# Constant products on TensorE, a gain loaded earlier, and another order of transposes in a two-block transformer kernel

## The chip, the cores and the metric

The kernel runs on one core of one Trainium2 chip. The time is that of the device for one execution, in microseconds (us); the time before is the median of 3 runs. A profile shows one execution: its span is the time from the first to the last instruction. Engines are named as in the profile: PE (TensorE, products), PEld (its weight loads), DVE (VectorE), ACT (ScalarE), POOL (GpSimd), SP (SyncE, which issues most transfers).

## The reference

256 tokens of width 1024 pass through two blocks of two layers each. The parts that matter here:

```python
def rms_norm(x, gain):
    xf = x.astype(jnp.float32)
    y = xf * lax.rsqrt(jnp.mean(xf * xf, axis=-1, keepdims=True) + NORM_EPS)
    return (y * gain.astype(jnp.float32)).astype(x.dtype)

def swiglu(h, w_gate, w_up, w_down):
    return (jax.nn.silu(h @ w_gate) * (h @ w_up)) @ w_down
...
def second_block(x, ...):
    for l in range(DEPTH):
        ...
        mix = jnp.concatenate([o_gla, o_rwkv, o_nsa], axis=-1) @ w_out[l]
        x = _layer_norm(DEEPNORM_ALPHA * x + mix, ln1_w[l], ln1_b[l])

        ffn = (jax.nn.silu(x @ ffn_w_gate[l]) * (x @ ffn_w_up[l])) @ ffn_w_down[l]
        x = _layer_norm(DEEPNORM_ALPHA * x + ffn, ln2_w[l], ln2_b[l])
    return x
```

The first block begins each layer with half a feed-forward (`x + swiglu(rms_norm(x)) / 2`), then a mixer and attention to a memory, then another half feed-forward. The second block has a mixer and a feed-forward per layer, each followed by a layer norm.

## The kernel before

x stays in SBUF as two tiles of 128 tokens (token half 0 and 1, `self.x[h]`), 1024 wide. Every product is taken in three: each f32 operand is split into a rounded part (`hi`) and the rest (`lo`). For weights, ACT writes `hi` (L159) and DVE `lo` (L160), one 512 KB tile at a time, out of four buffers that SP fills.

`norm_T` (L277) turns x into an operand. It takes x in four pieces, a token half h and a half i of the width; each piece is multiplied by the gain if there is one (L292), transposed by four PE transposes into one PSUM bank (L231), and split by ACT (L234) and DVE (L235). The order is i outside, h inside. Where there is a gain, ACT also sums squares (L300), and POOL takes the power that gives the root mean square (L244); the scaling itself comes after the product. `ffn1` (four calls, L365) and both mixers of block one call it with a gain; `ffn2` (two calls, L1041) and `mixer2` (two calls, L1114) call it without.

The very first thing that the program does with data is `ffn1(0, 0)`: `load_consts` (L380) issues the first part of the constants (identity and the exponent) on ACT's queue, `load_x` (L401) four loads of x on SP's, and `row_gain` (L247) two loads of the gain, spread over 128 partitions, through `load` (L172), which is POOL's queue at that point. Then come the feed-forward's weight tiles on SP's.

In block two, `post` (L1021) makes the layer norm: as the last product of each token half ends, DVE adds it to x (L1033) and takes statistics (L1035), then `ln` (L1007) makes the norm: DVE L1011 and L243, POOL's power L244, DVE L1016 twice, and DVE L1019 twice, of which each finishes one half of the width. Half 0 ends its last product first, so its norm runs under PE's products of half 1; the norm of half 1 has no products beside it. `swiglu` (L322) then takes the operand of both halves at once (256 columns, L480), 24 products to a weight tile; `dense` (L197) takes each token half by itself (512 columns, L217 to L219).

The order of every engine's queue is laid out by a planner that runs the program through a model, takes at each point the instruction that is ready and has the lowest priority number (`cur_priority`, counted up in program order), and gives out buffers. `later(n)` moves the instructions inside it n places back, and with a negative n forward; `norm_T` moves the two pieces with i = 0 forward by `AHEAD` = 150. On the chip each queue is then run in that order.

Of the kernel before, what the change touches and what calls it, by code (L numbers as in the profile page):

```python
# [18 lines left out]
AF = mybir.ActivationFunctionType  # L19
OP = mybir.AluOpType  # L20
# [4 lines left out]
def bcast_rows(ap, n, offset=0, parts=128):  # L25
    return bass.AP(tensor=ap.tensor, offset=ap.offset + offset, ap=[[0, parts], [1, n]])


class Core:
# [191 lines left out]
                    done(h, o)  # L221


    def split_T(self, src, nb, put):

        nc = self.nc
        for b0 in range(0, nb, 4):
            m = min(4, nb - b0)
            pt = self.p("t")
            for i in range(m):  # L230
                nc.tensor.transpose(pt[:, i * 128:(i + 1) * 128], src[:, (b0 + i) * 128:(b0 + i + 1) * 128], self.ident)  # L231
            v = pt[:, :m * 128].rearrange("p (b t) -> p b t", b=m)
            hi, lo = put(b0, m)
            nc.scalar.activation(hi, v, AF.Copy)  # L234
            nc.vector.tensor_tensor(lo, v, hi.bitcast(F32), op=OP.subtract)  # L235


    def rstd(self, ss, n, mean_scale, eps, r=None):
# [8 lines left out]
    def row_gain(self, ap, n):  # L247

        g = (self.kept("g1", 256) if n <= 256 else self.tagged("g4", 1024))[:, :n]
        for n0 in range(0, n, 512):  # L250
            self.load(g[:, n0:min(n, n0 + 512)], bcast_rows(ap, min(512, n - n0), n0))
        return g

    def operand(self, nb, groups=None):
# [19 lines left out]
        t = self.l(512)  # L274
        return [t[:, :256], t[:, 256:]]

    def norm_T(self, xs, gain, gates=True):  # L277


        nc = self.nc  # L280
        ahead = self.AHEAD if gates else 0
        with self.later(-ahead):
            put, get = self.operand(8, [("opX", 4)] * 2 if "opX" in self.caps[0] else None)
            ss = [self.t(2) for _ in range(2)]
        for i in range(2):

            with self.later(0 if i else -ahead):
                for h in range(2):
                    y = x = xs[h][:, 512 * i:512 * i + 512]
                    if gain is not None:  # L290
                        y = self.t(512)
                        nc.vector.tensor_tensor(y, x, gain[:, 512 * i:512 * i + 512], op=OP.mult)  # L292

                    old = self.bank
                    if "pC0" in self.caps[1]:
                        self.bank = f"C{2 * i + h}"
                    self.split_T(y, 4, lambda b, m: put(h, 4 * i + b, m))
                    self.bank = old
                    if gain is not None:
                        nc.scalar.activation(self.t(512), x, AF.Square, accum_out=ss[h][:, i:i + 1])  # L300
        if gain is not None:
            get.r = []
            for h in range(2):
                nc.vector.tensor_tensor(ss[h][:, :1], ss[h][:, :1], ss[h][:, 1:], op=OP.add)
                get.r.append(self.rstd(ss[h][:, :1], 1, 1.0 / 1024, 1e-6, self.l(1)))
            if gates:
                self.gate = self.pow
        return get
# [56 lines left out]
    def ffn1(self, layer, j):  # L365
        nc, I = self.nc, self.I
        gain = self.row_gain(I["ffn_norm"][layer, j], 1024)
        xT = self.norm_T(self.x, gain)
        half = [self.l(1) for _ in range(2)]
        for h in range(2):  # L370
            nc.vector.tensor_scalar(half[h], xT.r[h], 0.5, None, op0=OP.mult)

        def done(h, n0, ps):
            x = self.x[h][:, n0:n0 + 512]
            nc.vector.scalar_tensor_tensor(x, ps, half[h], x, op0=OP.mult, op1=OP.add)  # L375

        self.swiglu(xT, I["ffn_gu"][layer, j], I["ffn_w_down"][layer, j], done)


    def load_consts(self, cp):  # L380

        c = self.consts.tile([128, FIRST], F32, name="cf")
        self.nc.scalar.dma_start(c, cp[:, :FIRST])
        self.c = {k: c[:, a:a + n] for k, (a, n) in CONST_AT.items() if a < FIRST}
        self.ident = self.c["ident"]
        self.mhalf = self.c["mhalf"]

        self.ones = self.consts.tile([128, 160], F32, name="ones")[:, :128]
        self.nc.gpsimd.memset(self.ones, 1.0)

    def load_masks(self, cp, cb):

        c = self.consts.tile([128, CONST.shape[1] - FIRST], F32, name="cp")
        self.load(c, cp[:, FIRST:])
        b = self.consts.tile([128, CONST_B.shape[1]], BF, name="cb")
        self.load(b, cb)
        self.c.update({k: c[:, a - FIRST:a - FIRST + n] for k, (a, n) in CONST_AT.items() if a >= FIRST})
        self.cb = {k: b[:, a:a + n] for k, (a, n) in CONST_B_AT.items()}
        self.ident_b = self.cb["ident"]
# [69 lines left out]
FIRST = CONST_AT["ntri"][0]  # L469
# [535 lines left out]
class Mix2(Mix1):  # L1005
# [34 lines left out]

    def ffn2(self, layer):  # L1041
        I = self.I
        xT = self.norm_T(self.x, None)
        self.post("ln2", layer, "g2", lambda done: self.swiglu(
            xT, I["ffn_gu_2"][layer], I["ffn_w_down_2"][layer], done))

# [850 lines left out]
```

## Time and profile before

| | |
|---|---|
| median of 3 runs | 1983.48 us (1981.07 to 1987.65) |
| profiled execution | 1982.18 us, span 1980.5 us |
| mean granted TensorE clock | 0.985 of full speed |

How to read what follows: times are us from the start of the span. A row of the order of time gives the start, the duration (of all, where several are merged), the engine, the line, the operation, output and inputs, and in brackets how long the engine stood before it and who ended that. The granted clock is a share of 2.4 GHz; 0.50 is 1.2 GHz.

### The profile page before, as it was taken

The numbers are of one execution on the slowest core, as the hardware profiler recorded it, in microseconds if no ns is written. First come the engines' busy times: TensorE is split into PE (matmuls) and PEld (weight loads), VectorE is DVE, ScalarE is ACT, GpSimd is POOL, SyncE is SP. The second block draws the span as 40 slices with busy tenths as digits, with TensorE's granted clock in tenths as the row PEclk, the third lists the DMA queues.
The fourth block names the chain that finished last, engine by engine and source line by source line (L and its number), as shares of the span: only waits on it lengthen the run. The fifth ranks groups of instructions, "written<-read, shape, count | busy, mean of one in ns | idle before, by whom it ended". The sixth has DMA issues, their size and how long they took to land.

```text
span 1980.5 us, 35270 instructions
## 1 busy us (share of the span) xinstructions
PE 1896.3 (96%) x14108; PEld 1683.8 (85%) x14108; DVE 1249.6 (63%) x1999; ACT 995.6 (50%) x1611; POOL 189.9 (10%) x270
## 2 busy tenths in 40 slices
PE   7999999899999999898999999998999997998998
PEld 7998778799989987677999898777998885778996
DVE  5665865766566657766666557666555666665555
ACT  5544655555454545655554455543544464434542
POOL 0000401000000001320000013220000213210000
PEclk9999999999999999999999999999999998989999
DMA  6666443466556656224566654214666654015664
GB/s 231 193 215 223 141 145 106 128 197 194 193 198 192 193 191 201 95 100 139 164 196 194 205 152 140 96 44 144 197 193 193 173 158 132 23 64 180 193 192 138
DMA packets 158645, 319.17 MB, mean 161 GB/s; under 512 B 28944, under 2 KB 49680, under 8 KB 158480
## 3 DMA queue, kind: packets, MB, share of 16 engines
q1 hardware_dynamic: 157888, 315.79, 50.8%
q8 instruction: 111, 1.82, 0.4%
q0 software_dynamic: 160, 0.52, 0.1%
q10 hardware_dynamic: 432, 0.60, 0.1%
q14 instruction: 54, 0.44, 0.1%
HBM read 315.82 MB, written 1.05 MB: 160 GB/s over the span
## 4 chain that ended last, share of the span: by engine, by line
PE 48%; issue 4%; DVE 4%; ACT 1%; DMA 1%; POOL 0%; SPq 0%; DVEq 0%; POOLq 0%; ACTq 0%
PE pd L480 21%; PE pd L218 5%; PE pd L217 5%; PE pd L219 5%; PE po L480 2%; PE pr L480 1%; DVE wl L160 1%; PE ppC L480 1%; PE pr L1477 1%; PE pg L1247 1%; DMA wr<-in_ffn_w_down_dram 1%; PE pq L1477 1%; PE pg L480 1%; PE pt L516 1%; PE pn L480 1%
## 5 line engine op out<-in xcount | busy, mean ns | idle before, releaser
L160 DVE TENSOR_TENSOR wl<-wr,wh 128x1024 fp32r<-128x1024 f32 (+2 forms) x557 | 675.9, 1216 | 394.3 <-PE pd L218 127.4
L159 ACT ACTIVATE wh<-wr 128x1024 fp32r<-128x1024 f32 (+2 forms) x557 | 584.4, 1051 | 553.6 <-PE pd L480 200.8
L480 PE MATMUL pd<-opX,wl 128*128 128x256 f32 x2112 | 585.2, 278 | 2.4 <-DVE s L243 1.0
L480 PE MATMUL pd<-olX,wh 128*128 128x256 f32 x2112 | 585.3, 277 | 0.3 <-DVE olX L235 0.2
L480 PE MATMUL pd<-opX,wh 128*128 128x256 f32 x2112 | 584.5, 277 | 0.0
L480 PEld LDWEIGHTS pd<-opX,wl 128*128 128x128 f32 x2112 | 398.2, 189 | 3.3 <-ACT opX L234 2.2
L480 PEld LDWEIGHTS pd<-olX,wh 128*128 128x128 f32 x2112 | 398.5, 189 | 0.7 <-DVE olX L235 0.7
L480 PEld LDWEIGHTS pd<-opX,wh 128*128 128x128 f32 x2112 | 398.5, 189 | 0.0
L218 PE MATMUL pd<-wl,op 128*128 128x512 f32 (+4 forms) x952 | 366.2, 385 | 3.7 <-DVE wl L160 3.4
L219 PE MATMUL pd<-wh,op 128*128 128x512 f32 (+4 forms) x952 | 362.8, 381 | 0.0
L217 PE MATMUL pd<-wh,ol 128*128 128x512 f32 (+4 forms) x952 | 342.9, 385 | 3.9 <-DVE ol L235 2.9
L218 PEld LDWEIGHTS pd<-wl,op 128*128 128x128 f32 x952 | 179.7, 189 | 39.4 <-DVE wl L160 6.8
L217 PEld LDWEIGHTS pd<-wh,ol 128*128 128x128 f32 x952 | 178.6, 189 | 39.0 <-DVE ol L235 3.6
L219 PEld LDWEIGHTS pd<-wh,op 128*128 128x128 f32 x952 | 179.8, 189 | 32.2
L244 POOL TENSOR_TENSOR ls<-s,cf 128x1 f32<-128x1 f32 (+2 forms) x30 | 26.3, 879 | 719.9 <-DVE s L243 719.9
L357 DVE TENSOR_TENSOR b<-pd,b 128x256 f32<-128x256 f32 x132 | 55.9, 424 | 62.2 <-ACT b L356 44.2
L244 POOL TENSOR_TENSOR s<-s,cf 128x1 f32<-128x1 f32 (+2 forms) x22 | 22.4, 1018 | 441.1 <-DVE s L243 439.7
L356 ACT ACTIVATE b<-b 128x256 f32<-128x256 f32 x88 | 36.7, 418 | 46.6 <-DVE b L355 46.5
L361 DVE TENSOR_TENSOR ol<-b,op 128x512 fp32r<-128x512 f32 x66 | 45.4, 687 | 18.0 <-ACT op L360 18.0
L360 ACT ACTIVATE op<-b 128x512 fp32r<-128x512 f32 x66 | 41.7, 632 | 21.8 <-DVE b L357 21.1
L355 DVE TENSOR_TENSOR b<-pd,lb 128x256 f32<-128x256 f32 x88 | 37.1, 422 | 13.3 <-PE pd L480 13.3
L300 ACT ACTIVATE b<-x 128x512 f32<-128x512 f32 x32 | 20.2, 631 | 39.0 <-DVE x L375 20.9
(551 smaller groups left out, 2347.0 us busy)
## 6 DMA issues: line engine op xcount, KB each, us to landing
wr<-in_ffn_gu_dram SPq DMA_DIRECT2D x264, 512.0 KB, 4.2
wr<-in_ffn_w_down_dram SPq DMA_DIRECT2D x132, 512.0 KB, 3.7
wr<-in_w_in_dram SPq DMA_DIRECT2D x45, 512.0 KB, 4.1
wr<-in_ab_w_in_dram SPq DMA_DIRECT2D x24, 512.0 KB, 4.0
wr<-in_xm_w_kv_dram SPq DMA_DIRECT2D x16, 512.0 KB, 3.7
wr<-in_w_out_dram SPq DMA_DIRECT2D x16, 512.0 KB, 4.2
wr<-in_ab_w_out_dram SPq DMA_DIRECT2D x8, 512.0 KB, 3.6
wr<-in_xm_w_q_dram SPq DMA_DIRECT2D x8, 512.0 KB, 4.0
```

The costliest lines, as they stand in the source:

```text
L159: nc.scalar.activation(hi, raw, AF.Copy)
L160: nc.vector.tensor_tensor(lo, raw, hi.bitcast(F32), op=OP.subtract)
L217: nc.tensor.matmul(o, xl, wh[:, k], start=first, stop=False)
L218: nc.tensor.matmul(o, xh, wl[:, k], start=False, stop=False)
L219: nc.tensor.matmul(o, xh, wh[:, k], start=False, stop=last)
L244: self.pow = nc.gpsimd.tensor_tensor(r, a, self.mhalf[:, :n], op=OP.pow)
L355: nc.vector.tensor_tensor(s, ps[:, :256], R, op=OP.mult)
L357: nc.vector.tensor_tensor(y[:, b * 256:b * 256 + 256], ps[:, 256:], s, op=OP.mult)
L360: nc.scalar.activation(hi, yv, AF.Copy)
L361: nc.vector.tensor_tensor(lo, yv, hi.bitcast(F32), op=OP.subtract)
L480: i = self.k.nc.tensor.matmul(out, lhsT, rhs, start=start, stop=stop, skip_group_check=skip)
L1477: last = nc.tensor.matmul(out[rows(c), i], lhs[rows(c), i], rhs[rows(c), i], start=True, stop=True)
```

## The change

Three things change. First, the first call of `row_gain` issues its loads on ACT's queue, and the constants' first part is issued there between the gain's two loads, not ahead of them. Second, `norm_T` can be told to put products on PE whose results nobody reads: `busy` multiplies constants into a bank that is kept for it. The first norm gets 14 of them (`ones` times `ones`, 128 columns) at its start and 3 behind each of its four groups of transposes; `ffn2` gets 20 (identity times masks in bf16, 512 columns) behind its second group. They are put 20 places back in the plan, except for the 14, and each is laid behind the one before it on PE, the first of a group behind the last transpose. Third, where `norm_T` has no gain, in `ffn2` and `mixer2`, the pieces are taken with h outside and i inside, so that both of token half 0 come first, and it is these two that are moved forward by 150.

```diff
+    def busy(self, n, after=None):
+
+        nc = self.nc
+        for _ in range(n):
+            if self.idle_b:
+                i = nc.tensor.matmul(self.idle, self.ident_b, self.masks[:, :512], start=True, stop=True)
+            else:
+                i = nc.tensor.matmul(self.idle[:, :128], self.ones, self.ones, start=True, stop=True)
+            if after is not None:
+                self.tc.add_manual_dep(i.ins, after.ins.name,
...
+            after = i
...
     def row_gain(self, ap, n):
...
         for n0 in range(0, n, 512):
-            self.load(g[:, n0:min(n, n0 + 512)], bcast_rows(ap, min(512, n - n0), n0))
+            part, src = g[:, n0:min(n, n0 + 512)], bcast_rows(ap, min(512, n - n0), n0)
+            if self.first is None:
+                self.load(part, src)
+            else:
+
+                self.nc.scalar.dma_start(part, src)
+                if n0 == 0:
+                    self.first()
+        self.first = None
...
-    def norm_T(self, xs, gain, gates=True):
+    def norm_T(self, xs, gain, gates=True, fill=()):
...
-        for i in range(2):
-
-            with self.later(0 if i else -ahead):
-                for h in range(2):
...
+        fill = list(fill)
+        if fill:
+            self.idle = self.psum("d")
+            self.idle_b = gain is None
+            if gain is not None:
+                self.busy(fill.pop(0))
+
+        order = [(i, h) for i in range(2) for h in range(2)] if gain is not None else [(i, h) for h in range(2) for i in range(2)]
+        for n, (i, h) in enumerate(order):
+
+            with self.later(0 if n > 1 else -ahead):
...
+                last = self.split_T(y, 4, lambda b, m: put(h, 4 * i + b, m))
+                self.bank = old
+                if n < len(fill):
+                    with self.later(20):
+                        self.busy(fill[n], last)
...
-        xT = self.norm_T(self.x, gain)
+        xT = self.norm_T(self.x, gain, fill=(14, 3, 3, 3, 3) if layer + j == 0 else ())
...
-        self.nc.scalar.dma_start(c, cp[:, :FIRST])
+        self.first = lambda: self.nc.scalar.dma_start(c, cp[:, :FIRST])
...
+        self.masks = b
...
-        xT = self.norm_T(self.x, None)
+        xT = self.norm_T(self.x, None, fill=(0, 20))
```

## Rows read from the trace of the kernel before

**Rows 1.** The page, part 1: busy time, share of the span, instructions.
```profile
PE 1896.3 (96%) x14108; PEld 1683.8 (85%) x14108; DVE 1249.6 (63%) x1999; ACT 995.6 (50%) x1611; POOL 189.9 (10%) x270
```
**Rows 2.** The chain that ended last: start, duration, what; products of layer 1.
```profile
1791.13 121.06 PE pd L480 x1056
```
**Rows 3.** In order of time: the start, all engines, cut.
```profile
0.81 0.41 ACTq L383 DMA_DIRECT2D cf<-in_constants_dram  x1
...
0.82 1.81 SPq L405 DMA_DIRECT2D x<-in_x_dram  x4
...
1.36 1.30 POOL L173 DMA_DIRECT2D g<-in_ffn_norm_dram  x2 [0.34 <-issue]
2.67 3.20 SPq L141 DMA_DIRECT2D wr<-in_ffn_gu_dram  x4
3.77 0.63 ACT L300 ACTIVATE b<-x 128x512 f32<-128x512 f32 x1 [1.24 <-DMA x<-in_x_dram]
...
7.91 1.29 DVE L292 TENSOR_TENSOR b<-x,g 128x512 f32<-128x512 f32 x2 [6.73 <-DMA g<-in_ffn_norm_dram]
...
12.00 1.05 ACT L159 ACTIVATE wh<-wr 128x1024 fp32r<-128x1024 f32 x1
...
14.37 0.58 PE L480 MATMUL pd<-opX,wl 128*128 128x256 f32 x1 [0.64 <-DVE wl L160]
...
19.00 0.28 PE L480 MATMUL pd<-opX,wl 128*128 128x256 f32 x1
```
**Rows 4.** In order of time: block two's feed-forward, layer 0, cut.
```profile
1357.07 0.60 PE L231 MATMUL pt<-cf,x 128*128 128x128 f32 x4
...
1362.74 2.82 PE L231 MATMUL pt<-cf,x 128*128 128x128 f32 x12 [5.08 <-DVE x L1019]
1363.90 0.60 ACT L234 ACTIVATE opX<-pt 128x512 fp32r<-128x512 f32 x1 [5.09 <-PE pt L231]
1364.53 0.69 DVE L235 TENSOR_TENSOR olX<-pt,opX 128x512 fp32r<-128x512 f32 x1 [1.18 <-ACT opX L234]
...
1365.79 0.41 PE L480 MATMUL pd<-olX,wh 128*128 128x256 f32 x1
...
1367.27 0.28 PE L480 MATMUL pd<-opX,wh 128*128 128x256 f32 x1
```
**Rows 5.** Windows: stretch, length, busy per engine, clock, DMA share, GB/s.
```profile
1360.40:1360.60 0.20, 0.00 (x0) 0.00 (x0) 0.17 (x2) 0.00 (x0) 0.00 (x0) 0.55 0.83 307
```
**Rows 6.** In order of time: layer 1's third and fifteenth product, PE.
```profile
1791.36 0.41 PE L480 MATMUL pd<-olX,wh 128*128 128x256 f32 x1
...
1793.92 0.28 PE L480 MATMUL pd<-opX,wh 128*128 128x256 f32 x1
```
**Rows 7.** Landing after issue: first gain load, then first two weight tiles.
```profile
DMA to landing us min/median/max: 6.5/6.5/6.5
...
DMA to landing us min/median/max: 8.3/8.6/9.0
```
**Rows 8.** Windows of the start; the last two columns are DMA share, GB/s.
```profile
3.00:4.00 1.00, 0.00 (x0) 0.00 (x0) 0.00 (x0) 0.23 (x1) 0.00 (x0) 1.00 1.07 396
4.00:5.00 1.00, 0.00 (x0) 0.00 (x0) 0.00 (x0) 1.00 (x4) 0.00 (x0) 1.00 1.14 213
5.00:6.00 1.00, 0.00 (x0) 0.00 (x0) 0.00 (x0) 0.12 (x2) 0.00 (x0) 1.00 0.69 141
```
**Rows 9.** The chain that ended last, inside layer 1's norm of half 1.
```profile
1784.63 0.60 DVE olX L235
```
**Rows 10.** In order of time: mixer of block two, layer 1, cut.
```profile
1553.79 1.28 DVE L235 TENSOR_TENSOR ol<-pr,op 128x512 fp32r<-128x512 f32 x2
...
1554.94 0.48 PE L217 MATMUL pd<-wh,ol 128*128 128x512 f32 x1
```
**Rows 11.** Windows of block two's mixers: stretch, length, PE busy, and so on.
```profile
1136.00:1357.50 221.50, 212.47 (x2055) 175.16 (x2053) 145.88 (x325) 109.40 (x247) 50.50 (x76) 0.98 0.38 107
1547.00:1782.00 235.00, 217.08 (x2052) 178.07 (x2051) 152.43 (x334) 109.50 (x248) 53.47 (x80) 0.95 0.36 103
```

More of the change, by code (lines that the diff above doesn't have):

```diff
@@ L221, in dense @@
                     done(h, o)
+    idle = None
+    def busy(self, n, after=None):
[7 more added lines that the diff above has]
+                self.tc.add_manual_dep(i.ins, after.ins.name,
+                                       mybir.DependencyInfo(mybir.DependencyClass.NoSync, mybir.DependencyReason.DATA),
+                                       reason="while it would wait")
+            after = i
     def split_T(self, src, nb, put):
@@ L230, in split_T @@
             for i in range(m):
-                nc.tensor.transpose(pt[:, i * 128:(i + 1) * 128], src[:, (b0 + i) * 128:(b0 + i + 1) * 128], self.ident)
+                last = nc.tensor.transpose(pt[:, i * 128:(i + 1) * 128], src[:, (b0 + i) * 128:(b0 + i + 1) * 128], self.ident)
             v = pt[:, :m * 128].rearrange("p (b t) -> p b t", b=m)
@@ L235, in split_T @@
             nc.vector.tensor_tensor(lo, v, hi.bitcast(F32), op=OP.subtract)
+        return last
     def rstd(self, ss, n, mean_scale, eps, r=None):
@@ L284, in norm_T @@
             ss = [self.t(2) for _ in range(2)]
-        for i in range(2):
-            with self.later(0 if i else -ahead):
-                for h in range(2):
[L289 to L300, printed above, removed]
+        fill = list(fill)
[7 more added lines that the diff above has]
+            with self.later(0 if n > 1 else -ahead):
+                y = x = xs[h][:, 512 * i:512 * i + 512]
+                if gain is not None:
+                    y = self.t(512)
+                    nc.vector.tensor_tensor(y, x, gain[:, 512 * i:512 * i + 512], op=OP.mult)
+                old = self.bank
+                if "pC0" in self.caps[1]:
+                    self.bank = f"C{2 * i + h}"
+                last = self.split_T(y, 4, lambda b, m: put(h, 4 * i + b, m))
[3 more added lines that the diff above has]
+                        self.busy(fill[n], last)
+                if gain is not None:
+                    nc.scalar.activation(self.t(512), x, AF.Square, accum_out=ss[h][:, i:i + 1])
         if gain is not None:
```

## The prediction

> **What bounds the kernel now.** I read the page first: TensorE (PE) is busy for 96% of the span [rows 1], so only stretches in which it stands still, or runs slower than it can, are worth anything. Next came the list of who waited for whom, for PE alone: its longest waits are that for the first norm's product with the gain, and twice 5.1 us for the layer norm ahead of the second block's feed-forward. These three places are the ones that the change touches, and I read each in the order of time.
>
> *The start* [rows 3]. The first half of x is there at 3.77 us, when ScalarE (ACT) squares it. The gain's first half, issued by POOL at 1.36, is used by VectorE (DVE) at 7.91 only. The first real product starts at 14.37, behind the split of the first weight tile, which ACT begins at 12.00. Then 22 products start over the 4.63 us up to 19.00, 0.21 us apart; after that they come 0.115 us apart, as in the rest of the kernel, where 1056 take 121.06 us [rows 2]. So up to 19.00 PE runs at 1.2 GHz by its pitch and afterwards at 2.4, although the clock column shows 1.00 from the first slice on; here I go by the pitch.
>
> *The feed-forward of block two, layer 0* [rows 4]. PE transposes the first part of token half 0 at 1357.07 and then waits until 1362.74, because the next transposes in its queue belong to token half 1, whose norm ends last. In the pause the granted clock falls to half (0.55 over the slice at 1360.4 [rows 5]). Twelve transposes then take 2.82 us, and the products run 0.21 us apart until the tenth, at 1367.27. *Layer 1* is the same; its clock returns at the fifteenth product [rows 6].
>
> **The change, part by part.**
>
> *First norm's weight loaded first.* It moves two 256 KB loads from POOL's queue to ACT's, ahead of and behind the constants' first part. ACT then issues three transfers instead of one, 0.41 us each by the one row there is [rows 3], from 0.81 to about 2.05. Behind them it has a table load and then waits for x until 3.77 (1.24 us of waiting in that row), which covers the 0.8 us added; without that cover ACT would be 0.8 late. What the gain takes on ACT's queue no row shows. Bounds: x's first half, issued at 0.82 by SP, is used 2.95 us later; the gain on POOL's queue landed 6.5 us after its issue [rows 7]. I take 3.3, near x, which starts at the same time on the same kind of queue: the gain is there at 4.1 rather than 7.9.
>
> That doesn't yet start the products: the first weight tile landed 8.3 us after its issue at 2.67, at 11.0 [rows 7]. The DMA moved 396 GB/s in the fourth microsecond but 213 and 141 in the next two [rows 8], while POOL's two loads were under way. Were these two at 396, 0.44 MB or 1.1 us would be won: the tile lands at 9.9. If the loads are also served in the order of their need, 2.2 MB (x, gain, constants, tile) lie ahead; by an estimate 0.2 MB of it are moved by 3.0 us, and the rest at 396 GB/s is there at 8.0. I take the middle, 8.9. From the start of its split to the first product it is 2.37 us (12.00 to 14.37), so the first product is at 11.3: **-3.1 us**. Bounds: -1.0 if the tile lands at 11.0 as before (13.4), -3.5 if ACT's own work, four squares and two evictions at some 0.6 to 0.8 us behind a second half of x near 6 us, holds the split until 8.5.
>
> The Trainium skill (DMA: Bandwidth & Descriptors, section "Issuing engines are not separate DMA queues") speaks against a gain here: loads from all issuing engines share the same 16 DMA engines and interleave, so another queue saves issue time only. By it the tile would land at 11.0 and this part give the 1.0 us of the bound; the thin slices of rows 8 are why I don't take it whole.
>
> *Products of constants at the start.* 14 products of `ones` run as soon as POOL's memset is done, before POOL's next instruction at 1.36. The nearest row at the low clock is twelve 128-column f32 transposes in 2.82 us [rows 4], 0.23 each: 3.2 us, to 4.6. The first transposes can't start before 4.8 (gain 4.1, DVE's product 0.7), so the 14 lie in a wait. Four times 3 more follow the transposes, 2.8 us at the low clock, while PE waits for DVE and ACT; without that cover they would cost 0.7 a group. PE then works through most of 1.4 to 11 us. In rows 4 the clock came back 4.5 us after the first work behind the pause; so I expect 2.4 GHz before 11.3. The 22 products then take 22 x 0.115 = 2.5 us, not 4.63: **-2.1 us**; bounds 0 and -2.1.
>
> The Trainium skill (TensorE: Matmul & The Clock Gate, section "Part 4: PE-mode transpose") says that transposes don't count as work for the clock in the way products do. By it only the products of constants would work for the clock here, and the -2.1 us would be lost. In rows 4 the full clock came 1.5 us after the third product, in rows 6 2.6, both behind twelve transposes in a row; at the start, with transposes only thinly before, it came 4.6 us after the first. I read that as transposes that counted.
>
> *Token half 0 first, and 20 products behind it.* In the feed-forward PE now transposes both parts of half 0 (8 in about 1.1 us at full clock, to 1358.2), then runs 20 products of 512 columns. Such bf16 products have no row; by the 256-column pitch doubled each takes 0.23, together 4.6 us, to 1362.8. If each took half that, they end at 1360.5 and PE stands for 2.8 us, where the clock may fall and half of the gain below is lost. If each took twice that (half clock throughout) they overrun to 1367.4. I take 0.23, the nearest.
>
> What it costs: evicting the second part adds one DVE subtraction (L235) inside the layer norm of half 1. The chain of waits shows that norm as unbroken DVE work, with the first part's L235 in it at 0.60 us [rows 9]; one more puts 0.60 us on it, unless the planner places it behind. So the first x of half 1 is ready at 1363.3, after the products of constants. Four transposes at full clock end near 1363.9, ACT's eviction (0.60) at 1364.6, DVE's L235 (0.69) at 1365.3. The third product, the first that needs L235's output, starts at 1365.35 (1365.79 before), the tenth 7 x 0.115 later, at 1366.15 instead of 1367.27: -1.1. Layer 1, shifted alike: third at 1790.92 (1791.36), fifteenth 12 x 0.115 later at 1792.30 instead of 1793.92: -1.6. **Together -2.7 us**; bounds -3.9 (L235 behind the norm) and, should only the order work, about 0.
>
> *The mixers of block two* take the order without products of constants. In layer 1 two evictions came in one batch behind the layer norm: DVE's pair began at 1553.79, its first was done at about 1554.45, but PE had four more transposes queued and began at 1554.94 [rows 10]. With half 0 done early only half 1 is left there: **-0.4 us**, bounds -0.9 and +0.6 (L235 again). Layer 0 has no layer norm ahead: 0, bounds -0.6 and +0.6.
>
> One PSUM bank of the feed-forwards is held while the products of constants run; four or five others rotate two at a time, so this costs nothing, and one wait for a bank (up to a 0.4 us product) a group if they didn't.
>
> Sum: -3.1 - 2.1 - 2.7 - 0.4 = **-8.3 us**. Against the profiled execution (1982.18, of which the span is 1980.5) that is 1973.9; that execution lies 1.3 below the median of the runs, so I forecast 1983.5 - 8.3 = 1975.2, **1975** for the median.
>
> **Rivals.**
> - *The weights set the start* (the bound of rows 7): -1.0 there, so -6.2, 1977.3. For it: the weight tiles are three quarters of what the queues hold. Against: the two thin slices.
> - *The clock doesn't come earlier at the start*: -6.2, 1977.3 too. For it: between the groups PE still waits for DVE and ACT; against: rows 4 and 6, as read above.
> - *Products of constants don't hold the clock.* Identity times mask is mostly zeros, and no row shows whether such work counts. Then the clock falls at 1360.4 as before, ten of the 20 are left at 0.46 us, and PE is free at 1365.0 instead of 1362.74: +2.3. Eight transposes instead of twelve follow at 0.23, -0.9: +1.4 in each layer, and nothing from the clock at the start: -3.1 + 2.8 - 0.4 = -0.7, 1982.8, no change that shows.
> - *The planner's order turns worse: slower.* All queues are laid out by one plan over the whole program, and the mixers of block two now give other transposes the priority of 150 places. The two run nearly the same code, yet PE idles 9.0 us in layer 0's stretch and 17.9 in layer 1's [rows 11], so an order can cost up to 8.9 us. If both lost that once, +17.8 - 8.3 = +9.5, 1993.0. It decides from 8.3 us of new PE idle on. For it: this idle is all waits between short steps. Against: the edit inside these stretches is small.
>
> **How the numbers follow.** Chances: forecast 0.47, weights 0.17, clock at the start 0.14, clock not held 0.10, planner 0.12 (either way; slower in 0.07). The likeliest gives 1975. A measurement of this kernel tells about 0.3% (6 us) from no change. Faster: 0.41 of the forecast and half of the two rivals near -6 (0.16): 0.57. Slower: the planner's 0.07. Same: 0.36. The range goes from 1969 (all bounds at their best, -3.5 - 2.1 - 3.9 - 1.5 = -11.0, and 3 us for the scatter of a median) to 1982, which takes in both rivals near -6 and leaves out most of the last two.
>
> **What would show it.** Right: the gain's first use at 4 to 5 us; the first product of L480 near 11.3 and a pitch of 0.115 from there; the clock at 1.00 through both waits; one more L235 in the norm's chain; third products 0.4 us earlier. Wrong: a first weight tile at 11 us; a clock of 0.5 behind the 20 products; transposes of half 1 that stand behind products of constants; more PE idle in a mixer than in rows 11.

## The result, and the profile after

The forecast was 1975 us, range 1969 to 1982. Measured: a median of **1995.45 us** over 20 executions (1983.62 to 2006.28), beside 1984.8 us over 20 for the kernel before on the same chip (1979.21 to 1988.71): a ratio of 1.0053, 95% interval 1.0041 to 1.0065. The change makes the kernel slower by half a per cent, outside my range. Two later measurements of the same kernel gave 1.0031 (1.0012 to 1.0050) and 1.0024 (1.0007 to 1.0041): slower each time, by 4 to 11 us. The changed kernel's executions scatter over 23 us here, those of before over 10; in the two later measurements it is 14 and 13 us beside 20 and 13.

The profiled execution took 1999.06 us, span 1997.3, which is 16.8 us more than before's span. PE's part of the page, beside [rows 1]:

```profile
PE 1923.8 (96%) x14200; PEld 1705.4 (85%) x14200; DVE 1252.9 (63%) x1999; ACT 997.3 (50%) x1611; POOL 183.7 (9%) x268
```

PE is busy 27.5 us longer. The products of constants are some 18 us of that (6.3 for the first 14, some 3 for the next 12, and 2 x 4.5), so other work has become longer too.

*The start*, all engines in order of time, beside [rows 3]:

```profile
0.80 0.41 ACTq L274 DMA_DIRECT2D g<-in_ffn_norm_dram  x1
...
1.06 6.27 PE L233 MATMUL pd<-ones 128*128 128x128 f32 x28 [1.06 <-POOL ones L425]
...
5.29 1.42 DVE L325 TENSOR_TENSOR b<-x,g 128x512 f32<-128x512 f32 x2 [4.12 <-DMA g<-in_ffn_norm_dram]
...
7.17 0.60 PE L248 MATMUL pt<-cf,b 128*128 128x128 f32 x4
...
10.59 1.06 ACT L159 ACTIVATE wh<-wr 128x1024 fp32r<-128x1024 f32 x1
...
13.32 0.39 PE L517 MATMUL pd<-opX,wl 128*128 128x256 f32 x1
```

The gain is used at 5.29 instead of 7.91. The 14 products of constants show as 28 rows and last until 7.33, so that the first transposes wait for them. The first real product starts at 13.32 (14.37 before), and its 0.39 us instead of 0.58 (the row of the low clock in [rows 3]) says that the clock is already full.

*The feed-forward of block two, layer 0*: PE in order of time, beside [rows 4], and a window of it, beside [rows 5]:

```profile
1372.69 1.03 PE L248 MATMUL pt<-cf,x 128*128 128x128 f32 x8
1373.57 4.48 PE L231 MATMUL pd<-cb 128*128 128x512 bf16 x20
1378.96 1.38 PE L248 MATMUL pt<-cf,x 128*128 128x128 f32 x8 [0.92 <-DVE x L1056]
...
1381.03 0.39 PE L517 MATMUL pd<-olX,wh 128*128 128x256 f32 x1 [0.22 <-DVE olX L252]
...
1381.96 0.28 PE L517 MATMUL pd<-opX,wh 128*128 128x256 f32 x1
```
```profile
1377.00:1379.00 2.00, 1.08 (x6) 0.33 (x4) 2.00 (x4) 0.00 (x0) 1.00 (x1) 1.00 1.00 298
```

This place works as forecast: the wait of 5.08 us is 0.92, since 4.48 us of products of constants stand in it, the clock column stays at 1.00, and from the first transposes to the third and the tenth product it is 8.34 and 9.27 us, against 8.72 and 10.20 in [rows 4].

*Inside the feed-forwards* PE is never idle, and yet two of them have become longer. Windows of 80 us in the first one and the two of block two; the bracket behind PE's busy time counts the products:

```profile
40.00:120.00 80.00, 80.00 (x682) 80.00 (x681) 49.99 (x65) 40.00 (x50) 0.00 (x0) 1.00 0.60 187
1390.00:1470.00 80.00, 80.00 (x682) 80.00 (x681) 44.39 (x50) 40.72 (x51) 0.00 (x0) 1.00 0.60 188
1820.00:1900.00 80.00, 80.00 (x708) 80.00 (x707) 46.66 (x54) 41.83 (x55) 0.00 (x0) 1.00 0.61 193
```

682 products in 80 us are one in 117.3 ns, 708 one in 113.0. The same windows of before hold 709, 709 and 708. The clock column is 1.00 in all of them: there are two paces at one clock, which the prediction did not know of.

*The chain that ended last* gives the stretches between. Three pieces of before, then the same three of after; a piece is start, duration, what:

```profile
962.35 107.75 PE pd L480 x951
1365.57 120.56 PE pd L480 x1056
```
```profile
971.83 107.74 PE pd L517 x951
1381.03 124.41 PE pd L517 x1054
1809.91 119.74 PE pd L517 x1054
```

(The third of before is in [rows 2].) From the end of the first piece to the start of the second, the mixer of block two in layer 0 with its norm, it is 295.5 us before and 301.5 after, though the part from the norm's first transposes to the third product is 0.4 us shorter. So the loss has two parts: slow feed-forwards and longer mixers.

### The profile page after: what moved, and what is told of

The parts are those of the page before. It is cut to its first block, busy times and chain, and to the rows that moved or that the text cites. A ratio compares the mean times of both kernels' runs of the same rounds, so it can differ in the third digit from the quotient of the medians.

```text
span 1997.3 us, 35457 instructions
## 1 busy us (share of the span) xinstructions
PE 1923.8 (96%) x14200; PEld 1705.4 (85%) x14200; DVE 1252.9 (63%) x1999; ACT 997.3 (50%) x1611; POOL 183.7 (9%) x268
## 4 chain that ended last, share of the span: by engine, by line
PE 48%; issue 4%; DVE 4%; POOL 1%; ACT 1%; DMA 1%; SPq 0%; DVEq 0%; POOLq 0%; ACTq 0%
PE pd L517 21%; PE pd L217 5%; PE pd L218 5%; PE pd L219 5%; PE po L517 2%; PE pr L517 1%; PE ppC L517 1%; PE pr L1514 1%; DVE wl L160 1%; PE pg L1284 1%; PE pq L1514 1%; PE pg L517 1%; PE pn L517 1%; PE pt L553 0%; PE pq L794 0%
```

## The experiments

Theory A: the products of constants at the start change the planner's order in mixers far behind them, and that costs what is lost. Theory B: the two paces are settled anew in each execution, whatever the kernel. Their rivals stand with each run. The instruction lists of the builds can be compared without the chip: against before, the loads alone change no engine's order behind the first norm. The loads with the 26 products of constants move instructions in the mixers near 250, 860 and 1240 to 1340 us, although no line of code there was touched. The order in which the instructions start in the traces says the same. By that order (it does not tell the pieces of x apart) block two's part alone moves one product near 1145 us and nothing else ahead of layer 0's norm at 1357 us; behind that it moves many, above all from 1665 to 1760 us. e5, e7 and e12 have one list from the first norm on.

The table has the stretches of each trace in us, worked out from the order of time: from the first to the last product of a feed-forward that reads `opX`, and the time between one and the next. "Start" ends with the first product; ff1 is the first feed-forward, ff5 and ff6 those of block two; m0, m1 are the mixers of block one, m2 and m3 those of block two, norms included. The other three feed-forwards are within 0.3 us in all and left out.

| kernel | start | ff1 | m0 | m1 | m2 | ff5 | m3 | ff6 | ratio to before |
|---|---|---|---|---|---|---|---|---|---|
| before | 14.4 | 122.3 | 258.8 | 256.6 | 288.9 | 120.6 | 304.9 | 121.1 | |
| after | 13.3 | 124.8 | 263.4 | 259.6 | 294.5 | 124.9 | 304.0 | 120.2 | 1.0053 |
| e1_again | 12.6 | 120.2 | 260.7 | 258.2 | 296.3 | 120.2 | 305.3 | 120.2 | 1.0031 |
| e2_loads | 12.2 | 122.0 | 261.2 | 254.4 | 289.1 | 120.3 | 304.5 | 121.2 | 0.9984 |
| e3_start | 12.6 | 120.2 | 260.0 | 258.8 | 296.9 | 120.6 | 302.7 | 120.6 | 1.0019 |
| e4_ffn | 13.6 | 121.1 | 260.3 | 257.2 | 288.6 | 120.2 | 302.1 | 120.2 | 0.9976 |
| e5_both | 12.7 | 122.0 | 262.4 | 255.6 | 292.3 | 120.2 | 305.8 | 124.8 | 0.9982 |
| e6_busy_old_loads | 14.6 | 120.2 | 259.7 | 255.8 | 289.1 | 120.4 | 305.7 | 125.3 | 1.0007 |
| e7_four | 12.0 | 126.2 | 261.0 | 253.1 | 288.5 | 120.2 | 301.5 | 124.8 | 0.9975 |
| e8_order_alone | 15.0 | 127.4 | 262.4 | 256.2 | 289.1 | 120.6 | 311.6 | 121.2 | 1.0056 |
| e11_after_again | 12.3 | 120.2 | 260.8 | 257.1 | 297.3 | 120.2 | 303.0 | 120.2 | 1.0024 |
| e12_four_again | 12.2 | 121.9 | 262.4 | 253.1 | 288.5 | 120.2 | 301.7 | 120.2 | 0.9968 |

**e1_again: the changed kernel, unaltered.** No edit.

> The changed kernel unaltered, a second time. Theory A: the two parts of the loss (products 118 instead of 113 ns apart in the first feed-forward and in block two's feed-forward of layer 0; longer mixers, whose instructions stand in another order) belong to the program, so the trace shows the same places again: both streams at 117 to 118 ns, the stretches of mixers within 1 us of the first trace, median 1995. Rival B: the pitch is settled anew in each execution; then another set of the six feed-forwards is slow in this trace (a slow one costs 4.7 us), with the same order of instructions.

Median 1989.94 us, ratio 1.0031 (1.0012 to 1.0050), profiled execution 1988.47. The mixers are long again (m2 296.3), if not within the 1 us that A gave; the feed-forwards are not. The first two of the windows above:

```profile
40.00:120.00 80.00, 80.00 (x709) 80.00 (x708) 51.03 (x65) 40.79 (x51) 0.00 (x0) 1.00 0.62 195
1390.00:1470.00 80.00, 80.00 (x709) 80.00 (x708) 45.61 (x51) 40.69 (x52) 0.00 (x0) 1.00 0.63 196
```

So A holds for the mixers and B for the pace: one program ran the first feed-forward at 682 products in one execution and at 709 in another. Each slow feed-forward costs some 4.7 us (124.9 against 120.2), so such changes may make a part of the scatter; no run shows how large a part.

**e2_loads: only the loads.**

```
-        xT = self.norm_T(self.x, gain, fill=(14, 3, 3, 3, 3) if layer + j == 0 else ())
+        xT = self.norm_T(self.x, gain, fill=())
...
-        order = [(i, h) for i in range(2) for h in range(2)] if gain is not None else [(i, h) for h in range(2) for i in range(2)]
+        order = [(i, h) for i in range(2) for h in range(2)]
...
-        xT = self.norm_T(self.x, None, fill=(0, 20))
+        xT = self.norm_T(self.x, None)
```

> Only the loads in the new order; no products of constants, transposes in the old order. Every engine's order of instructions behind the first norm is then that of before. Theory A: the first weight tile sets the start, -1.0 us there, nothing elsewhere: 1984 beside 1985 for before. Rival (my forecast's step): the tile lands 2.1 us earlier, -3.1 us. Rival B: the stretch lengths of the mixers are as before, but feed-forwards may be slow at random, up to +4.7 each.

Median 1981.22 us, ratio 0.9984 (0.9966 to 1.0002). The start, in order of time, and the landing time of the first weight tile alone (issued at 2.66), beside [rows 7], where it is the 8.3:

```profile
4.87 0.63 ACT L336 ACTIVATE b<-x 128x512 f32<-128x512 f32 x1 [1.37 <-DMA x<-in_x_dram]
...
9.80 1.06 ACT L159 ACTIVATE wh<-wr 128x1024 fp32r<-128x1024 f32 x1
...
12.22 0.58 PE L517 MATMUL pd<-opX,wl 128*128 128x256 f32 x1 [0.29 <-DVE wl L160]
```
```profile
DMA to landing us min/median/max: 7.1/7.1/7.1
```

The first tile now lands at 9.8 instead of 10.9, and ACT begins its split at once, at 9.80; before, the tile had lain there for 1.1 us when ACT came to it, at 12.00. Together that is the 2.15 us by which the first product starts earlier: between the 1.0 that theory A gave and the 3.1 of the forecast. x itself comes 1.1 us later (3.77 before). One start is one draw: in the eight traces with the gain on ACT's queue the tile lands at 9.2 to 10.3 and the first product starts at 12.0 to 13.3, in the four with the old loads at 10.9 to 11.5 and 13.6 to 15.0. The whole time doesn't clear the noise.

**e3_start: loads and products of constants at the start.** The second and third edit of e2 alone.

> The loads and the products of constants at the start, nothing in block two. By the build, the products of constants alone change the order of instructions in the mixers near 250, 860 and 1260 to 1340 us. Theory A: the start -1.0, the first feed-forward slow +2.5, the mixers near 250 and 860 us longer as in the changed kernel (+4.6 and +3.0), a part of the +5.6 near 1300 us: 1992 to 1996. Rival (the order is harmless, block two loses all): 1983.

Median 1988.19 us, ratio 1.0019 (1.0002 to 1.0036): less than theory A gave, which had counted a slow first feed-forward (+2.5) and a longer m0 (+4.6), and neither is in this trace. With ff1 at 120.2, m1 and m2 are 2 and 8 us longer than before, with block two's code untouched. The rival is out: the median is 7 us above that of e2, on the same chip.

**e4_ffn: block two's part alone.** `row_gain` and `load_consts` as before, and the first edit of e2.

> Only block two's part: token half 0 first and the 20 products of constants; loads and start as before. The order of instructions is that of before until 1240 us. Theory A: until then all as before; the mixer of block two in layer 0 up to 3 us longer, its feed-forward slow (+4.2), layer 1 faster (-1.8): 1987 to 1990. Rival (block two's part works as forecast, the loss is all from the start): -2.7, 1982.

Median 1981.31 us, ratio 0.9976 (0.9959 to 0.9994): the rival, my forecast's step, was right. m2 + ff5 + m3 + ff6 come to 831.1 us instead of 835.5. Some 2.4 us of these 4.4 arise at the two norms, as forecast (0.9 and 1.5, below); the rest is in m3, whose order the planner changed.

**e5_both: loads and block two's part, no products at the start.** Only the first edit of e2.

> The changed kernel without its products of constants at the start: the loads and block two's part alone, each 3 to 5 us faster than before by itself. Theory A (the products at the start cost what they cost through the order of the mixer of block two, layer 0): that stretch back to 288 to 290 us instead of 294 to 297, no half clock of 10 us near 1255 and 1340; the two gains add up: 7 us faster than before, ratio 0.9965. Rival (the two parts hinder one another): no faster than either alone, 0.998.

Median 1980.03 us, ratio 0.9982 (0.9964 to 1.0000). The traced execution has one slow feed-forward (124.8) and an m2 of 292.3, longer than A gave but under the 294.5 to 297.3 of the four traces with the changed order. The traced execution is the slowest of the twelve (1991.00 us), and the lists are those of e7 below, whose m2 is 288.5; the same stretch of m2, e5 and then e7, shows why the two differ:

```profile
1143.00:1146.00 3.00, 3.00 (x8) 2.32 (x7) 0.68 (x2) 0.00 (x0) 0.00 (x0) 0.50 0.76 5
```
```profile
1143.00:1146.00 3.00, 3.00 (x17) 2.54 (x16) 1.72 (x2) 1.39 (x2) 0.00 (x0) 1.00 0.26 2
```

In e5 the granted clock falls to 0.50 here and once more near 1273 us, in e7 it doesn't. So at one order a mixer can differ by some 4 us from execution to execution. The median gains 5 us, not 7: by this run alone it is not settled whether the two parts add up.

**e6_busy_old_loads: the 26 products at the start, the gain on POOL's queue.** `row_gain` and `load_consts` as before, and the last two edits of e2.

> The same 14 and 12 products of constants at the start, but the two loads of the gain stay on POOL's queue; block two as before. By the build this changes the order of instructions in the mixer near 250 us only; near 860 and 1240 to 1340 us it is that of before. Theory A (order): the stretch of the mixer of block two, layer 0 is 289 us, with 7 us of half clock near 1255 and none near 1340; 1983 to 1985, as before. Rival C (the products of constants themselves make the clock fall later on, whatever the order): that stretch is 296 us with two falls of 10 us, 1990.

Median 1985.52 us, ratio 1.0007 (0.9991 to 1.0023). m2 is 289.1. This pair settles it: e3 and e6 run the same products of constants, e2 and e3 the same loads; only where both together have changed the order is m2 long. (The planner gives out the buffers together with the order, and no run separates these two.) The chain's pieces, first of e3, then of e6:

```profile
962.04 107.75 PE pd L517 x951
1373.27 120.50 PE pd L517 x1056
```
```profile
961.03 107.75 PE pd L517 x951
1364.46 120.35 PE pd L517 x1056
```

303.5 us against 295.7 from piece to piece. What the order does is seen best at the end of m2: PE in order of time with the changed order (the trace of e11, the changed kernel) and with the old one (e6).

```profile
1335.12 1.00 PE L517 MATMUL po<-lb2N,b2N 128*128 128x64 f32 x8
1338.31 1.11 PE L248 MATMUL pq<-cf,b2N 128*128 128x128 f32 x4 [2.19 <-POOL b2N L1852]
1341.83 0.66 PE L248 MATMUL pg<-cf,b1G 128*128 128x128 f32 x2 [2.41 <-DVE b1G L1316]
1343.42 0.79 PE L217 MATMUL pd<-wh,lb2G 128*128 128x512 f32 x1 [0.93 <-DVE lb2G L252]
```
```profile
1334.57 0.48 PE L217 MATMUL pd<-wh,lb2G 128*128 128x512 f32 x1
...
1336.97 0.66 PE L248 MATMUL pq<-cf,b2N 128*128 128x128 f32 x4 [0.75 <-POOL b2N L1852]
1338.05 0.50 PE L218 MATMUL pd<-wl,op 128*128 128x512 f32 x1 [0.43 <-DVE wl L160]
```

In the old order the last tile of one of the three branches (`b1G`) is finished early, and the output projection's products that read it (`lb2G`) fill PE while another branch's last tile (`b2N`) is on its way. In the changed order both tiles come last, one behind the other, and PE has nothing left: 2.19 + 2.41 + 0.93 us. The windows, e11 and then e6, show what comes on top:

```profile
1335.00:1345.00 10.00, 4.47 (x20) 3.27 (x20) 5.92 (x19) 1.36 (x3) 2.27 (x2) 0.64 0.00 0
1345.00:1350.00 5.00, 5.00 (x17) 3.98 (x16) 2.45 (x2) 2.12 (x2) 0.00 (x0) 0.69 0.33 97
```
```profile
1335.00:1345.00 10.00, 8.83 (x40) 6.75 (x39) 6.68 (x7) 3.78 (x4) 1.28 (x1) 1.00 0.36 107
1345.00:1350.00 5.00, 5.00 (x24) 4.05 (x23) 2.73 (x4) 1.06 (x1) 0.00 (x0) 1.00 0.65 204
```

In all four traces with the changed order the granted clock is at 0.50 for some 10 us at this place, and for some 10 us near 1255; in the eight others for 6.8 us near 1255 and not here at all. In e11's first window it is 0.64 on average, and even the next 5 us, with PE never idle, hold 17 products instead of 24. Products put in to keep the clock up at the start and at the norms have cost the clock here.

**e7_four: loads, block two's part, 4 products at the start.** By the build the order is that of e5.

```
-        xT = self.norm_T(self.x, gain, fill=(14, 3, 3, 3, 3) if layer + j == 0 else ())
+        xT = self.norm_T(self.x, gain, fill=(4,) if layer + j == 0 else ())
```

> The loads, block two's part, and 4 products of constants at the start instead of 14 and 12. By the build the order behind the first norm is that of the kernel without any. Theory A: the mixer of block two, layer 0 at 289 us; the clock at the start rises between 6 us (14 products) and 16 us (none), worth up to 1.5 us: 7 to 8.5 us faster than before. Rival C (the products themselves): that stretch longer by some part of 7 us.

Median 1980.23 us, ratio 0.9975 (0.9959 to 0.9990): 5 us faster than before, not the 7 to 8.5 that theory A gave; A's m2 (288.5) holds. The trace has two slow feed-forwards (ff1 and ff6).

**e8_order_alone: token half 0 first, no products of constants at all.** The edits of e4, and the last of e2.

> Only the order of transposes in block two (token half 0 first), with no products of constants at all and the old loads. If the 20 products hold the clock, then without them the half clock of 7 us behind each layer norm's wait is back (near 1360 and 1790 us), each feed-forward starts 1 to 2 us later than with them, and the time is that of before less about 1: 1984. Rival (the order alone makes the gain): 1981, as with the 20 products.

Median 1995.14 us, ratio 1.0056 (1.0035 to 1.0078): both expectations missed. The clock does fall behind the norm again, as the first said; PE in order of time and a window:

```profile
1372.62 1.94 PE L248 MATMUL pt<-cf,x 128*128 128x128 f32 x8 [5.32 <-DVE x L1056]
```
```profile
1373.00:1375.00 2.00, 2.00 (x10) 1.66 (x8) 0.76 (x2) 1.00 (x2) 0.00 (x0) 0.50 0.48 183
```

But the planner answers this edit with an order of m3 that costs 6.7 us (311.6), and the traced execution had a slow first feed-forward. So the 20 products are not only what holds the clock: with them in the plan the mixer of layer 1 happens to come out well (302.1 in e4). e4's gain belongs to the pair, not to the order.

**e9_break and e10_break_again: one product of constants ahead of each later group of 96 products.** On e5; `broken` is set at the end of the first feed-forward, so that the three behind it stay as they are:

```
             chains = [Chain(self) for _ in banks]
+            if g and not (hasattr(xT, "r") and self.broken):
+                chains[0].last = self.nc.tensor.matmul(banks[0][:, :128], self.ones, self.ones, start=True, stop=True)
```

> Theory B says that the pitch of a feed-forward (113.3 or 117.8 ns) is settled by chance when its row of products begins, and kept until PE is interrupted. Here the loads and block two's part stand without products of constants at the start, and one product of constants stands ahead of each of the ten later groups of 96 products in the first feed-forward and the two of block two, 30 in all, some 0.1 to 0.25 us each. Theory B: within one feed-forward some groups run at 113 and some at 118. Rival (something that lasts, such as where operands lie, or a clock finely set): all eleven groups of one feed-forward have one pitch. The mixers' order of instructions is changed by this too, so its whole time says nothing.

> The same kernel as the one with breaks, once more, for 30 more groups. Theory B: other groups are slow than in its first trace. Rival (settled by what stands in the program): the same groups are slow.

2006.07 and 2002.69 us, one execution each. Windows inside four successive groups of the first feed-forward, e9 and then two of them in e10:

```profile
41.00:51.00 10.00, 10.00 (x87) 10.00 (x86) 5.75 (x9) 4.31 (x6) 0.00 (x0) 1.00 0.54 169
52.00:62.00 10.00, 10.00 (x91) 10.00 (x90) 6.03 (x9) 4.71 (x6) 0.00 (x0) 1.00 0.54 185
63.00:73.00 10.00, 10.00 (x88) 10.00 (x87) 6.07 (x8) 4.72 (x6) 0.00 (x0) 1.00 0.58 197
75.00:85.00 10.00, 10.00 (x90) 10.00 (x90) 6.01 (x9) 4.37 (x6) 0.00 (x0) 1.00 0.56 176
```
```profile
41.00:51.00 10.00, 10.00 (x88) 10.00 (x87) 5.63 (x8) 4.23 (x7) 0.00 (x0) 1.00 0.54 165
52.00:62.00 10.00, 10.00 (x90) 10.00 (x89) 6.03 (x9) 4.56 (x6) 0.00 (x0) 1.00 0.58 182
```

87, 91, 88, 90 products in 10 us: slow, fast, slow, fast. By the starts of all products, the mean distance in successive groups is 113.3, 117.8, 113.3, 117.8 ns and so on: the pace turns over at each of the 28 products of constants in a trace that have ten or more products at full clock on either side (the other two, first in block two's feed-forwards, have only two ahead of them), and the same groups are slow in both traces, as the rival of the second run said. Theory B was right that the pace can change inside a feed-forward, and wrong that chance decides at each break: here it is a state with two values that one such product turns over.

**e11_after_again and e12_four_again: the changed kernel and e7's, on one chip.** No new edits.

> The changed kernel a third time, beside the best candidate on the same chip. Theory A and B: mixer of block two, layer 0 at 294 to 297 us again; of the feed-forwards only those behind a norm at the start and in block two can be slow; ratio to before 1.003 to 1.005.

> Loads, 4 products of constants at the start, and block two's part, beside the changed kernel on the same chip. Theory A: mixer of block two, layer 0 at 289 us; ratio to before 0.996 to 0.9985, and 10 us faster than the changed kernel.

1988.06 us, ratio 1.0024 (1.0007 to 1.0041), and 1976.47 us, ratio 0.9968 (0.9954 to 0.9982): 11.6 us apart. m2 is 297.3 against 288.5, as A said; neither trace has a slow feed-forward.

## Why the prediction was wrong, step by step

**The step that failed is the planner's, the fourth rival.** The sum has no term for a changed order outside the edited places: it takes it as nothing. I looked for a worse order only in the mixers of block two, only from the edit inside them, which I called small, and gave it 0.07 on the slow side. But it was the 26 products of constants at the start that went into the plan, and the plan of the whole program shifted. In the four traces with that order m2 is 294.5 to 297.3 (mean 296.3), in the eight others 288.5 to 292.3 (mean 289.3): +7.0. m1 is 257.1 to 259.6 (mean 258.4) against 253.1 to 257.2 (mean 255.3): +3.2. m0, whose order they also change, shows no difference. Together +10 us, m1's part of it less sure than m2's, since its two ranges touch. With the gains below, some -6 us, that leaves the +4 of the two later medians. The rival's price of 17.8 less 8.3 for both layers, +9.5, came near by accident: its second half never came (m3 is 303.0 to 305.3 in the changed kernel, 304.9 before).

**The loads** were sized at -3.1 and gave -2.15 (e2). What was mis-sized is the first tile's landing: I took the middle, 8.9, between 9.9 (the two thin slices filled) and 8.0 (loads served in the order of need), and it landed at 9.8. That this is near the 9.9 is luck:

```profile
3.00:4.00 1.00, 0.00 (x0) 0.00 (x0) 0.00 (x0) 0.50 (x1) 0.00 (x0) 1.00 0.88 182
4.00:5.00 1.00, 0.00 (x0) 0.00 (x0) 0.00 (x0) 0.13 (x1) 0.00 (x0) 1.00 0.94 291
5.00:6.00 1.00, 0.00 (x0) 0.00 (x0) 0.81 (x2) 0.72 (x3) 0.00 (x0) 1.00 1.03 332
```

In e2 the two slices that were thin in [rows 8] did fill, but the one ahead of them emptied: 0.81 MB from 3 to 6 us beside 0.75 MB before, not the 0.44 MB more that I had counted. The bound that I named, ACT's own work behind a late x, did not hold the split: it began as the tile landed. The gain was used at 5.1 to 5.4 where I had 4.1. My reading that the weight tiles are three quarters of what the queues hold was too high: four tiles of 512 KB stand beside 1 MB of x and 0.5 MB of gain, a little over half. In the changed kernel the products of constants take part of this back: from the start of the split to the first product it is 2.7 to 3.0 us in the five traces with the 26 of them and 2.4 in the seven others. Each shows as two rows of 0.22 us where I had priced one row of 0.23, so the first 14 take 6.3 us instead of 3.2 and last past the gain's arrival. The Trainium skill (DMA: Bandwidth & Descriptors, section "Issuing engines are not separate DMA queues") would have left the tile where it was; the trace of e2 has it 1.1 us earlier. That does not yet speak against it, because the order of the requests changed too: SP issued the second tile at 5.1 instead of 3.2. What in that order brings the first tile forward was not tried by itself.

**The clock at the start**: forecast -2.1; ff1 is 120.2 in the traces with 26 products and no slow pace, 122.3 before and 121.1 to 122.0 in the others without slow pace. So it came, at up to its full size. With no products of constants (e2), and with 4 of them (e12, below), the first product is still at the low clock:

```profile
12.21 0.58 PE L517 MATMUL pd<-opX,wl 128*128 128x256 f32 x1 [0.29 <-DVE wl L160]
```

(That is e12; e2's row stands above.) In both, PE had done sixteen transposes before it. That agrees with the Trainium skill (TensorE: Matmul & The Clock Gate, section "Part 4: PE-mode transpose"), by which transposes don't count for the clock as products do, better than with my reading of [rows 4, 6], that they counted. It doesn't decide it, because the sixteen came in bursts with pauses between them.

**Block two's feed-forwards**: forecast -1.1 and -1.6. In layer 0 the tenth product comes 0.93 us earlier, counted from the first transposes (9.27 against 10.20; 9.26 in e4); in layer 1 the fifteenth comes 1.5 us earlier (9.81 against 11.28). The one more L235 in the norm shows at its price of 0.60: half 1's first transposes come 6.27 us behind half 0's instead of 5.67. The 20 products took 4.48 us (forecast 4.6), and PE waited 0.92 behind them (forecast 0.5) at full clock. Right, and the third rival, that constants don't hold the clock, is out. *The mixers of block two*, forecast -0.4: in layer 1 the two batches of transposes hold PE up 0.2 us less in e4 than before. What the plan does to the rest of m3 (301.5 to 311.6 us by kernel) is far larger, so this term can't be read from a whole time.

**Not foreseen at all** was the slow pace, worth 9.3 us in the first trace (ff1 and ff5) and nothing in the second and third. It is also where the code is that of before (ff6 in e6, ff1 in e8), so it is not charged to the change; whether the change alters its odds is open. With 7 slow ones among 36 (ff1, ff5, ff6 of twelve traces) and none among the other 36, twelve traces can't tell. A median of 20 executions of the one program came out at 1995.45 and two of 12 at 1989.94 and 1988.06; I take the later two, 4 to 5 us above before, for what the order costs net of the gains. That is a choice: of the first 20 only one was traced, and why their median lies 5 to 7 us above the later ones stays open.

## What to carry to other kernels

Where one planner lays out the whole program, filler work is part of the plan: compare the instruction lists of the two builds outside the place that was edited before pricing anything, since 26 products in the second microsecond moved work 1.2 ms later and cost 10 us where they had won 2 at most. Prefer the filler that leaves the lists alone: 4 products instead of 26, with the same loads and the same 20 products behind the norms, ran 5 to 8 us faster than before. Whether the 4 add anything is not shown: with none of them (e5) it was 5 us too. And before a difference of a few us is explained, count the products per window in the long streams of more than one trace.

## What was not expected of the hardware

A stream of weight loads and 256-column products ran at one of two paces at the same granted clock of 1.00: one product in 113.3 or in 117.8 ns (709 or 682 in 80 us), 4 per cent apart. The pace held for a whole feed-forward of some 1050 products in block two, differed from execution to execution of one program, and turned over with each single 128-column f32 product of constants set between, 56 times of 56 in two traces. It is not every interruption that does this: in e12's second feed-forward four transposes turn it from 118 to 113 ns and the four rows of the products that spread the norm's factors, behind them (L354), leave it there, and in its fourth the transposes turn it from 113 to 118 and those rows turn it back. Three of the six feed-forwards, all of block one, were at 113.3 from those rows on in every trace, with some 20 to 25 products at 118 ahead of them; the first, which has such rows too, ran at either pace. What sets the pace at the beginning of a stream stays open.

A 128-column f32 product of constants showed as two rows of 0.22 us at the low clock, twice as much as the transpose of the same shape in [rows 4] (0.23).
